# One pair of FFN columns fewer multiplied plainly, and the row scale's work queued ahead of the combinations

## The chip, the cores and the metric

One core of a Trainium2 chip. The time is in device microseconds (us), from start to end of one execution; the median of 3 runs counts. A profiled execution gives the trace.

## What is computed

One decoder layer, 512 tokens, width 1024, all in f32. The change touches the two half-step FFNs and the projection between them:

```python
h = h + 0.5 * swiglu(rms_norm(h, ln_ffn1), w1_gate, w1_up, w1_down)     # DFF = 2816
u = rms_norm(h, ln_mix) @ w_in                                          # recurrence and attention
h = h + concat([o_hgrn, o_mla]) @ w_out
h = h + 0.5 * swiglu(rms_norm(h, ln_ffn2), w2_gate, w2_up, w2_down)
h = h + sigmoid(rms_norm(h, ln_ple) @ w_ple_gate) * (p @ w_ple_proj)
y = rms_norm(h, ln_final)

def rms_norm(x, g): return x * rsqrt(mean(x * x) + 1e-6) * g            # per token
def swiglu(x, wg, wu, wd): return (silu(x @ wg) * (x @ wu)) @ wd
```

## The kernel before

**Layout and precision.** h lies transposed: 8 tiles of 128 features by 512 tokens. Every f32 factor is split into an upper half (ScalarE copies it to fp32r) and the rest (VectorE subtracts); a product is three matmuls, hi*hi, lo*hi, hi*lo (`mm3`, L226). Weights come from HBM in pieces of 8 blocks of 128x128 (`WStream`): 7 buffers for raw pieces (tag `wraw`), 3 for split ones (`whi`, `wlo`). L73 makes the upper half of a piece on ScalarE, L74 the rest on VectorE. A load goes out on SyncE when its buffer is free.

**Norm.** `Norm.add` (L295) scales a tile of h by the gain and splits it (L238, L239). `square` (L302) squares it on ScalarE and adds it to a running sum on VectorE. The factor per token is applied only after the product: `finish` (L327) sums over the features with four tiny matmuls (L268, tile `ss`) and takes the reciprocal root with a dozen 4-wide VectorE operations (`rsqrt_of`, L241 to L262). `row_bcast` (L343) spreads it: a diagonal, upper half (L275) and rest (L280), two matmuls with ones (L282, L283), and a copy to SBUF (L346, tile `rb`).

**FFN.** There are 22 column tiles of 128, taken in pairs. A plain pair is four products of gate and up columns, each of 8 slices of x of 3 matmuls of 512 columns, 96 in all. `plain_out` (L366) then forms gate times factor (L368), silu (L369), times up (L371), and splits it (L235, L236). A Strassen pair treats gate and up, two halves of the features and two halves of the tokens as a 2x2 block product, with 7 products (`product`, L374) of 24 matmuls of 256 columns. Its operands are combinations of weights (`_form`: T1 L101, T2 L104, T3 L107, T4 L110, on VectorE, 1024 wide) and of x (`forms`, L311: for each k from 0 to 3 one ScalarE copy, four VectorE operations L317 to L320, and two splits into tiles `sx`). `end_pair` (L402) collects them; c is read on VectorE at L416 before its second use (L382).

PSUM has three accumulators `acc`, three `t` and two `aux`. The first FFN computes three pairs plainly, the second two, and the rest by Strassen (`PLAIN`, L1045). After six pairs the first `down` follows, after eleven the second.

The opening of an FFN: tiles 0 and 1 (four accumulators `gu`) take the slices of x in the order MO; then come `finish`, tile 2 in steps of two slices, `row_bcast` after six of the eight, `plain_out` for tiles 0 and 1, and with the later tiles one or two of the groups of combinations. Tile 3's accumulators are those of tile 0, so its first matmul waits until VectorE has read the gate of tile 0 (L368), and its second accumulator until L371. In the first FFN the squares are taken after the loop over the slices (L559); in the second with each tile of h that w_out finishes (L946).

The order of the program is a Python program's. The framework's scheduler then moves instructions on each engine, by its own estimate of when they are ready; each engine runs its own list in order.

Of the kernel before, what the change touches and what calls it, by code (L numbers as in the profile page):

```python
# [10 lines left out]
F32 = mybir.dt.float32  # L11
# [3 lines left out]
AF = mybir.ActivationFunctionType  # L15
ALU = mybir.AluOpType
# [5 lines left out]
KD = D // P  # L22
# [9 lines left out]
MO = [0, 4, 1, 5, 2, 6, 3, 7]  # L32
# [7 lines left out]
class WStream:  # L40
# [104 lines left out]
    def next(self, n=1):  # L145
        if not self.left:
            self._fill()
            self.left = self.ready.pop(0)
        hi, lo, o, end = self.left[0]
        assert o + n <= end  # L150
        self.left = self.left[n:]
        s = slice(o * P, (o + n) * P)
        return hi[:, s], lo[:, s]
# [10 lines left out]
def block_kernel(ctx: ExitStack, tc: tile.TileContext, xT, pT, pos, wst, items, vecs, lnf, cmask, tmask, out):  # L164
    nc = tc.nc
    V, S, G, PE = nc.vector, nc.scalar, nc.gpsimd, nc.tensor
# [9 lines left out]
    def nm(s):  # L176
        count[0] += 1
        return f"{s}_{count[0]}"

    def slot(name, dt=F32):  # L180
        return slots.tile([P, T], dt, tag="slot", name=nm(name), bufs=NSLOT)

    def tmpt(name, tag="tmp", bufs=4):
        return tmp.tile([P, T], F32, tag=tag, name=nm(name), bufs=bufs)

    def acc(name):
        return ps.tile([P, T], F32, tag="acc", name=nm(name), bufs=3)

    def tps(name):
        return ps.tile([P, T], F32, tag="t", name=nm(name), bufs=3)  # L190

    def aslot(name, dt=F32):
        return slots.tile([P, T], dt, tag="a", name=nm(name), bufs=8)

    def aux(name):
        return ps.tile([P, T], F32, tag="aux", name=nm(name), bufs=2)
# [8 lines left out]
    ones = const.tile([P, 1], F32, name="ones")  # L205
# [6 lines left out]
    warm = const.tile([P, 1], F32, name="warm")  # L212
    S.activation(warm, ones, AF.Silu)
    ident = const.tile([P, P], F32, name="ident")
# [49 lines left out]
    def col_sums(sqs, out):  # L264

        for j in range(sqs[0].shape[1] // P):
            for i, sq in enumerate(sqs):
                PE.matmul(out[:, j:j + 1], sq[:, j * P:(j + 1) * P], ones,  # L268
                          start=(i == 0), stop=(i == len(sqs) - 1))

    def broadcast_ps(r):

        n = r.shape[1]
        hi, lo = (tmp.tile([P, T], F32R, tag="tmp", name=nm("dg"), bufs=4) for _ in range(2))
        V.tensor_tensor(hi[:, :n * P].rearrange("p (j t) -> p j t", j=n),  # L275
                        ident.unsqueeze(1).broadcast_to([P, n, P]),
                        r.unsqueeze(2).broadcast_to([P, n, P]), op=ALU.mult)
        for j in range(n):
            c = slice(j * P, (j + 1) * P)
            V.scalar_tensor_tensor(lo[:, c], ident, r[:, j:j + 1], hi[:, c].bitcast(F32), op0=ALU.mult, op1=ALU.subtract)  # L280
        b = aux("rbp")
        PE.matmul(b[:, :n * P], ones_r, hi[:, :n * P], start=True, stop=False)  # L282
        PE.matmul(b[:, :n * P], ones_r, lo[:, :n * P], start=False, stop=True)  # L283
        return b
# [58 lines left out]
    def row_bcast(r, tag):  # L343
        b = broadcast_ps(r)
        o = tmpt("rb", tag=tag, bufs=1) if tag == "rb" else slot(tag)
        S.activation(o, b, AF.Copy)  # L346
        return o

    def ffn(norm, next_norm, n_plain, first=None, extra=None):

# [2 lines left out]
        rb = None  # L355

        def gated(f, tmp_a):
            new = aslot if f % 12 < 4 else slot
            hi, lo = new("ah", F32R), new("al", F32R)
            if len(tmp_a.shape) == 3:  # L360
                split(tmp_a, hi.rearrange("p (two t) -> p two t", two=2), lo.rearrange("p (two t) -> p two t", two=2))
            else:
                split(tmp_a, hi, lo)
            a_hi[f], a_lo[f] = hi, lo

        def plain_out(f, g, u):  # L366
            gs = tmpt("gs")
            V.tensor_tensor(gs, g, rb, op=ALU.mult)  # L368
            S.activation(gs, gs, AF.Silu)  # L369
            a = tmpt("a")  # L370
            V.tensor_tensor(a, u, gs, op=ALU.mult)  # L371
            gated(f, a)
# [67 lines left out]
                if last:  # L440
                    next_norm.add(m)

        if first is None:
            first = [acc("gu"), tps("gu"), acc("gu"), tps("gu")]
            for k in MO:
                for u in first:
                    mm3(u, W.next(), norm.x(k), k == MO[0], k == MO[-1])
        g, u = acc("gu"), tps("gu")

        def plain_tile(n=KD):  # L450

            for i, k in enumerate(MO):
                for o in (g, u):
                    mm3(o, W.next(), norm.x(k), k == MO[0], k == MO[-1])
                if i % n == n - 1:
                    yield

        tile2 = plain_tile(2)
        r = norm.finish()
        S.activation(warm, ones, AF.Silu)  # L460
        for _ in range(3):
            next(tile2)
        rb = row_bcast(r, "rb")
        next(tile2)
        for f in range(2):
            plain_out(f, first[2 * f], first[2 * f + 1])
        forms = list(range(4))
        for f in range(2, 2 * n_plain):
            if f > 2:
                next(plain_tile())  # L470
            if forms:
                norm.forms(forms.pop(0))
            if n_plain == 2:
                norm.forms(forms.pop(0))
            plain_out(f, g, u)
            if f + 1 < 2 * n_plain:
                g, u = acc("gu"), tps("gu")
        d = {}
        begin = start_pair(d)
        for _ in begin:  # L480
# [70 lines left out]

    n1 = Norm(V_LN1)
    first = [acc("gu"), tps("gu"), acc("gu"), tps("gu")]
    for k in MO:
        n1.add(k, square=False)
        for u in first:
            mm3(u, W.next(), n1.x(k), k == MO[0], k == MO[-1])
    W.ahead = 3
    for k in range(KD):  # L559
        n1.square(k)  # L560
    nmix = Norm(V_LNM)
    ffn(n1, nmix, PLAIN[0], first, make_tables)
    cos, sin, lb, oml = (tables[n] for n in ("cos", "sin", "lb", "oml"))


# [11 lines left out]
    rb = rc = None  # L577
# [215 lines left out]
    rb = row_bcast(rc, "rb")  # L793
# [146 lines left out]
    n2 = Norm(V_LN2)  # L940
    for m in MO:
        u = acc("wo")
        for k in range(KD):
            mm3(u, W.next(), mix[k], k == 0, k == KD - 1)
        V.tensor_tensor(h[m], h[m], u, op=ALU.add)
        n2.add(m)  # L946


    n3 = Norm(V_LNP)
    ffn(n2, n3, PLAIN[1])  # L950


    pp = []
    for j in range(2):
        praw = aslot("praw")
        nc.sync.dma_start(praw, pT[j * P:(j + 1) * P, :])
        hi, lo = aslot("ph", F32R), aslot("pl", F32R)
# [84 lines left out]


GROUPS = {}
PLAIN = (3, 2)  # L1045
FORMS = ("T1", "B11", "B21", "T2", "T3", "B22", "T4")


def _stream(w1_gate, w1_up, w1_down, w_in, w_q_up, w_kv_up, w_out, w2_gate, w2_up, w2_down, w_ple_gate, w_ple_proj):
# [19 lines left out]
    def col(n):  # L1069
        return slice(n, n + P)  # L1070

    def ffn(n, g, u, d, sizes):
        plain([w[k * P:(k + 1) * P, col(f * P)] for k in MO for f in range(2) for w in (g, u)], sizes)
        plain([w[k * P:(k + 1) * P, col(f * P)] for f in range(2, 2 * PLAIN[n]) for k in MO for w in (g, u)])
        first = n * KF
        for p in range(PLAIN[n], KF // 2):
            GROUPS[first + p] = {
# [8 lines left out]

        forms(PLAIN[n], "T1", "B11")
        for p in range(PLAIN[n], KF // 2):
            forms(p, "B21", "T2")
# [90 lines left out]
```

## Time and profile before

| | us |
|---|---|
| median of 3 runs | 1024.57 (1023.31 to 1025.12) |
| profiled execution | 1024.24 |
| its span | 1022.5 |
| TensorE busy | 1007.6 |
| VectorE busy | 728.6 |
| ScalarE busy | 449.5 |

The span is counted from the first to the last instruction; all starts below are in us from its start. Busy times overlap between engines. Matmuls are pipelined, so one lasts longer in the list than the distance to the next: the distance is the cost. DVE is VectorE, ACT ScalarE, PE TensorE, PEld its weight loads, SP SyncE.

### The profile page before, as it was taken

To read this page: it belongs to the slowest core of one execution; us is meant where nothing else is said; L and a number is where in the kernel's file an instruction comes from. 1 tells how busy PE (TensorE), PEld (TensorE's weight loads), DVE (VectorE), ACT (ScalarE), POOL (GpSimd) and SP (SyncE) were. 2 spreads that over 40 slices of the span, in tenths; PEclk is the share of its full clock that TensorE was granted. 3 is DMA by queue.
4 is the path that set the end of the run, shared out by engine and by line. 5 is a ranking of instruction groups with operands and counts; after the bars stand their busy time and mean duration, and the time that the engine had idled before them with its cause. 6 is when DMAs were issued, how large, how long until landed. Compare 5 with 4: busy or idle time off the path is not lost.

```text
span 1022.5 us, 14842 instructions
## 1 busy us (share of the span) xinstructions
PE 1007.6 (99%) x5987; PEld 885.0 (87%) x5987; DVE 728.6 (71%) x1183; ACT 449.5 (44%) x694; POOL 4.6 (0%) x13
## 2 busy tenths in 40 slices
PE   9899999999999999999999999999999999999996
PEld 7789998899998888897777788999988999988885
DVE  7857975579877668765757667788744699766655
ACT  8435552145554332345544444555521355543443
POOL 0000000000000000000000000000000000000000
PEclk9999999999999999999999999999999999999998
DMA  8212353123344321222310222132432223443301
GB/s 332 63 62 83 89 170 110 62 83 104 108 142 126 99 93 52 73 78 68 104 62 1 76 89 83 42 120 88 146 102 83 83 83 104 138 136 98 103 21 62
DMA packets 28980, 97.68 MB, mean 96 GB/s; under 512 B 3456, under 2 KB 3456, under 8 KB 28912
## 3 DMA queue, kind: packets, MB, share of 16 engines
q1 hardware_dynamic: 28752, 96.25, 29.2%
q8 instruction: 47, 0.77, 0.3%
q0 software_dynamic: 160, 0.49, 0.2%
q14 instruction: 21, 0.17, 0.0%
HBM read 94.10 MB, written 2.10 MB: 94 GB/s over the span
## 4 chain that ended last, share of the span: by engine, by line
PE 93%; DVE 3%; issue 1%; DMA 1%; ACT 1%; SPq 0%; DVEq 0%; ACTq 0%
PE down L228 8%; PE down L229 8%; PE down L230 8%; PE a L384 6%; PE a L383 6%; PE a L382 6%; PE c L382 3%; PE c L384 3%; PE c L383 3%; PE gu L228 3%; PE gu L229 3%; PE gu L230 3%; PE b L384 2%; PE b L383 2%; PE b L382 2%; PE ufq L228 2%
## 5 line engine op out<-in xcount | busy, mean ns | idle before, releaser
L73 ACT ACTIVATE whi<-wraw 128x1024 fp32r<-128x1024 f32 (+1 forms) x220 | 230.1, 1046 | 388.4 <-PE down L229 85.7
L74 DVE TENSOR_TENSOR wlo<-wraw,whi 128x1024 fp32r<-128x1024 f32 (+1 forms) x220 | 265.1, 1205 | 85.1 <-ACT whi L73 84.3
L229 PE MATMUL down<-al,whi 128*128 128x512 f32 x352 | 137.1, 390 | 0.0
L228 PE MATMUL down<-ah,whi 128*128 128x512 f32 x352 | 137.1, 390 | 0.0
L230 PE MATMUL down<-ah,wlo 128*128 128x512 f32 x352 | 137.0, 389 | 0.0
L382 PE MATMUL c<-sx,whi 128*128 128x256 f32 x272 | 78.7, 289 | 0.6 <-DVE u L416 0.6
L228 PEld LDWEIGHTS down<-ah,whi 128*128 128x128 f32 x352 | 66.1, 188 | 14.2 <-ACT ah L235 0.7
L229 PEld LDWEIGHTS down<-al,whi 128*128 128x128 f32 x352 | 66.1, 188 | 13.7 <-DVE al L236 0.4
L230 PEld LDWEIGHTS down<-ah,wlo 128*128 128x128 f32 x352 | 66.1, 188 | 13.7
L384 PE MATMUL a<-x,wlo 128*128 128x256 f32 x272 | 77.0, 283 | 0.0
L384 PE MATMUL a<-sx,wlo 128*128 128x256 f32 x272 | 77.0, 283 | 0.0
L383 PE MATMUL a<-sx,whi 128*128 128x256 f32 x272 | 77.0, 283 | 0.0
L383 PE MATMUL a<-x,whi 128*128 128x256 f32 x272 | 77.0, 283 | 0.0
L382 PE MATMUL a<-sx,whi 128*128 128x256 f32 x272 | 77.0, 283 | 0.0
L384 PE MATMUL c<-sx,wlo 128*128 128x256 f32 x272 | 76.9, 283 | 0.0
L382 PE MATMUL a<-x,whi 128*128 128x256 f32 x272 | 76.9, 283 | 0.0
L383 PE MATMUL c<-sx,whi 128*128 128x256 f32 x272 | 76.9, 283 | 0.0
L228 PE MATMUL gu<-x,whi 128*128 128x512 f32 x160 | 63.5, 400 | 2.9 <-DVE gs L368 2.6
L229 PE MATMUL gu<-x,whi 128*128 128x512 f32 x160 | 62.9, 394 | 0.0
L230 PE MATMUL gu<-x,wlo 128*128 128x512 f32 x160 | 62.7, 393 | 0.0
L382 PEld LDWEIGHTS c<-sx,whi 128*128 128x128 f32 x272 | 52.0, 191 | 3.2 <-DVE u L416 2.6
L383 PEld LDWEIGHTS a<-x,whi 128*128 128x128 f32 x272 | 52.2, 192 | 0.1
(308 smaller groups left out, 2173.5 us busy)
## 6 DMA issues: line engine op xcount, KB each, us to landing
wraw<-wst SPq DMA_DIRECT2D x169, 512.0 KB, 3.4
h<-xT SPq DMA_DIRECT2D x8, 256.0 KB, 6.1
out<-y SPq DMA_DIRECT2D x8, 256.0 KB, 2.2
wraw<-wst SPq DMA_DIRECT2D x7, 256.0 KB, 2.7
rpb<-rpa SPq DMA_DIRECT2D x8, 64.0 KB, 2.1
praw<-pT SPq DMA_DIRECT2D x2, 256.0 KB, 3.4
gf<-lnf SPq DMA_DIRECT2D x2, 256.0 KB, 4.3
posi<-pos POOLq DMA_DIRECT2D x1, 256.0 KB, 4.3
```

The source lines that it names most:

```text
L73: self.nc.scalar.activation(hi, src, AF.Copy)
L74: self.nc.vector.tensor_tensor(lo, src, hi.bitcast(F32), op=ALU.subtract)
L228: PE.matmul(out, a[0], b[0], start=start, stop=False)
L229: PE.matmul(out, a[0], b[1], start=False, stop=False)
L230: PE.matmul(out, a[1], b[0], start=False, stop=stop)
L382: PE.matmul(o, hi[:, c], x[0], start=begin and i == 0 and k == 0, stop=False, skip_group_check=True)
L383: PE.matmul(o, hi[:, c], x[1], start=False, stop=False, skip_group_check=True)
L384: PE.matmul(o, lo[:, c], x[0], start=False, stop=end and i == 1 and k == 3, skip_group_check=True)
```

## The change

One pair more in each FFN goes by Strassen (`PLAIN` from (3, 2) to (2, 1)), 19 in place of 17. In the first FFN each tile's square is taken with the tile, the row sums come before the last slice, and the first group of combinations right behind them; the broadcast comes after four slices of tile 2, and groups 1 to 3 follow the outputs of tiles. In the second FFN the row sums come after one slice, the broadcast after six, still in tiles 0 and 1; three groups of combinations are made in w_out, after the tiles of h that they need, and the fourth behind the scale. `tc.issue_after` keeps those groups behind the last VectorE operation of the broadcast's diagonal in VectorE's list.

```diff
         for j in range(n):
             c = slice(j * P, (j + 1) * P)
-            V.scalar_tensor_tensor(lo[:, c], ident, r[:, j:j + 1], hi[:, c].bitcast(F32), op0=ALU.mult, op1=ALU.subtract)
+            chain_end[0] = V.scalar_tensor_tensor(lo[:, c], ident, r[:, j:j + 1], hi[:, c].bitcast(F32), op0=ALU.mult, op1=ALU.subtract)
...
-        if first is None:
-            first = [acc("gu"), tps("gu"), acc("gu"), tps("gu")]
-            for k in MO:
+        def behind(k):
+
+            with tc.issue_after(chain_end[0].ins):
+                norm.forms(k)
+
+        S.activation(warm, ones, AF.Silu)
+        if n_plain == 1:
+            first, forms = [acc("gu"), tps("gu"), acc("gu"), tps("gu")], [3]
+            for i, k in enumerate(MO):
+                if i == 1:
+                    r = norm.finish()
+                if i == 6:
+                    rb = row_bcast(r, "rb")
                 for u in first:
                     mm3(u, W.next(), norm.x(k), k == MO[0], k == MO[-1])
-        g, u = acc("gu"), tps("gu")
-
-        def plain_tile(n=KD):
-
+        else:
+            forms = [1, 2, 3]
+        for f in range(2, 2 * n_plain):
+            g, u = acc("gu"), tps("gu")
             for i, k in enumerate(MO):
+                if f == 2 and i == 4:
+                    rb = row_bcast(r, "rb")
+                    for e in range(2):
+                        plain_out(e, first[2 * e], first[2 * e + 1])
+                    behind(forms.pop(0))
                 for o in (g, u):
                     mm3(o, W.next(), norm.x(k), k == MO[0], k == MO[-1])
-                if i % n == n - 1:
-                    yield
-
-        tile2 = plain_tile(2)
-        r = norm.finish()
-        S.activation(warm, ones, AF.Silu)
-        for _ in range(3):
-            next(tile2)
-        rb = row_bcast(r, "rb")
-        next(tile2)
-        for f in range(2):
-            plain_out(f, first[2 * f], first[2 * f + 1])
-        forms = list(range(4))
-        for f in range(2, 2 * n_plain):
-            if f > 2:
-                next(plain_tile())
+            plain_out(f, g, u)
             if forms:
-                norm.forms(forms.pop(0))
-            if n_plain == 2:
-                norm.forms(forms.pop(0))
-            plain_out(f, g, u)
-            if f + 1 < 2 * n_plain:
-                g, u = acc("gu"), tps("gu")
+                behind(forms.pop(0))
+        if n_plain == 1:
+            behind(forms.pop(0))
+            for e in range(2):
+                plain_out(e, first[2 * e], first[2 * e + 1])
...
-    for k in MO:
-        n1.add(k, square=False)
+    for i, k in enumerate(MO):
+        n1.add(k)
+        if i == KD - 1:
+            r1 = n1.finish()
+            n1.forms(0)
         for u in first:
             mm3(u, W.next(), n1.x(k), k == MO[0], k == MO[-1])
     W.ahead = 3
-    for k in range(KD):
-        n1.square(k)
...
         n2.add(m)
+        if 4 <= m < 7:
+            n2.forms(m - 4)
...
-PLAIN = (3, 2)
+PLAIN = (2, 1)
```

TensorE's list at the end of tiles 0 and 1 of the first FFN, before (x_253 is the last slice of x, x_126 the first, here of tile 2):

```order
L230 MATMUL gu_124<-x_253,wlo_238 128x512
L228 MATMUL gu_125<-x_253,whi_237 128x512
L229 MATMUL gu_125<-x_253,whi_237 128x512
L230 MATMUL gu_125<-x_253,wlo_238 128x512
L268 MATMUL ss_293<-ones,ssum_268 128x1 x4
L228 MATMUL gu_291<-x_126,whi_317 128x512
```

and now (x_249 is the last slice but one, x_273 the last):

```order
L230 MATMUL gu_125<-x_249,wlo_258 128x512
L268 MATMUL ss_279<-ones,ssum_129 128x1 x4
L228 MATMUL gu_122<-x_273,whi_257 128x512
L229 MATMUL gu_122<-x_273,whi_257 128x512
L230 MATMUL gu_122<-x_273,wlo_258 128x512
L228 MATMUL gu_123<-x_273,whi_257 128x512
```

The row sums moved from behind the last slice to ahead of it.

VectorE's list in the first FFN from the end of the reciprocal root (ry) over the two diagonals (dg) to the first gate product (gs), before:

```order
L257 SCALAR_TENSOR_TENSOR ry_300<-ru_303,ry_300 128x4
L317 SCALAR_TENSOR_TENSOR sf_678<-h_78,vec,a_77_677 128x256
L74 TENSOR_TENSOR wlo_360<-wraw_357,whi_359 128x1024
L275 TENSOR_TENSOR dg_375<-ident,ry_300 128x512
L101 TENSOR_TENSOR wraw_619<-wraw_615,wraw_617 128x1024
L280 SCALAR_TENSOR_TENSOR dg_376<-ident,ry_300,dg_375 128x128 x4
L318 SCALAR_TENSOR_TENSOR sf_678<-h_74,vneg,sf_678 128x256
L319 SCALAR_TENSOR_TENSOR sf_678<-h_74,vec,a_77_677 128x256
L320 SCALAR_TENSOR_TENSOR sf_678<-h_78,vec,sf_678 128x256
L74 TENSOR_TENSOR wlo_446<-wraw_443,whi_445 128x1024
L368 TENSOR_TENSOR gs_399<-gu_122,rb_385 128x512
```

and now:

```order
L257 SCALAR_TENSOR_TENSOR ry_286<-ru_289,ry_286 128x4
L277 TENSOR_TENSOR dg_372<-ident,ry_286 128x512
L74 TENSOR_TENSOR wlo_345<-wraw_342,whi_344 128x1024
L282 SCALAR_TENSOR_TENSOR dg_373<-ident,ry_286,dg_372 128x128 x4
L319 SCALAR_TENSOR_TENSOR sf_403<-h_76,vec,a_47_402 128x256
L321 SCALAR_TENSOR_TENSOR sf_403<-h_72,vec,a_47_402 128x256
L320 SCALAR_TENSOR_TENSOR sf_403<-h_72,vneg,sf_403 128x256
L107 TENSOR_TENSOR wraw_473<-wraw_591,wraw_473 128x1024
L322 SCALAR_TENSOR_TENSOR sf_403<-h_76,vec,sf_403 128x256
L236 TENSOR_TENSOR sx_410<-sf_403,sx_409 128x512
L74 TENSOR_TENSOR wlo_420<-wraw_417,whi_419 128x1024
L370 TENSOR_TENSOR gs_384<-gu_122,rb_382 128x512
```

Between ry and the second diagonal stood a combination (sf), a weight piece (L74) and a formed weight (L101); now one piece does. The combinations, T3 (L107) and a piece stand between it and the gate product.

VectorE's list at the end of w_out, from the residual add of the last tile but one (h_74), before (x_5555 is the last x, its sum follows):

```order
L945 TENSOR_TENSOR h_74<-h_74,wo_5485 128x512
L74 TENSOR_TENSOR wlo_5527<-wraw_5524,whi_5526 128x1024
L239 SCALAR_TENSOR_TENSOR x_5517<-h_74,vec,x_5517 128x512
L309 TENSOR_TENSOR ssum_5293<-ssum_5293,sq_5520 128x512
L945 TENSOR_TENSOR h_78<-h_78,wo_5523 128x512
L74 TENSOR_TENSOR wlo_5568<-wraw_5565,whi_5567 128x1024
L239 SCALAR_TENSOR_TENSOR x_5555<-h_78,vec,x_5555 128x512
L309 TENSOR_TENSOR ssum_5293<-ssum_5293,sq_5558 128x512
```

and now (x_5696 is the last x, rv_5730 the first operation of the reciprocal root):

```order
L947 TENSOR_TENSOR h_74<-h_74,wo_5626 128x512
L236 TENSOR_TENSOR sx_5623<-sf_5612,sx_5622 128x512
L74 TENSOR_TENSOR wlo_5668<-wraw_5665,whi_5667 128x1024
L239 SCALAR_TENSOR_TENSOR x_5658<-h_74,vec,x_5658 128x512
L311 TENSOR_TENSOR ssum_5389<-ssum_5389,sq_5661 128x512
L947 TENSOR_TENSOR h_78<-h_78,wo_5664 128x512
L107 TENSOR_TENSOR wraw_5788<-wraw_5927,wraw_5788 128x1024
L239 SCALAR_TENSOR_TENSOR x_5696<-h_78,vec,x_5696 128x512
L311 TENSOR_TENSOR ssum_5389<-ssum_5389,sq_5699 128x512
L74 TENSOR_TENSOR wlo_5710<-wraw_5707,whi_5709 128x1024
L247 TENSOR_SCALAR rv_5730<-ss_5725 128x4
```

A low half (sx) came in ahead of the piece, T3 of the first Strassen pair (L107) came ahead of the last x, and a weight piece moved behind its sum.

## Rows read from the trace of the kernel before

**Rows 1.** The page, busy time, share of the span and instructions of each engine.
```profile
PE 1007.6 (99%) x5987; PEld 885.0 (87%) x5987; DVE 728.6 (71%) x1183; ACT 449.5 (44%) x694; POOL 4.6 (0%) x13
```

**Rows 2.** Waits of TensorE, whole span: us in total, times, longest.
```profile
PE gu L228 <- DVE gs L368: 2.6, 1, 2.6
...
PE c L382 <- DVE u L416: 0.6, 1, 0.6
```

**Rows 3.** TensorE timeline, first FFN: start, length, line, operation, idle before.
```profile
28.13 0.94 PE L268 MATMUL ss<-ones,ssum 128*128 128x1 f32 x8
...
28.93 0.49 PE L228 MATMUL gu<-x,whi 128*128 128x512 f32 x1
...
40.72 0.40 PE L230 MATMUL gu<-x,wlo 128*128 128x512 f32 x1
...
43.70 0.50 PE L228 MATMUL gu<-x,whi 128*128 128x512 f32 x1 [2.59 <-DVE gs L368]
...
78.11 0.28 PE L382 MATMUL c<-sx,whi 128*128 128x256 f32 x1
```

**Rows 4.** Stages: length; busy us (count) of PE, PEld, DVE, ACT, POOL; clock, DMA, GB/s.
```profile
5.00:20.00 15.00, 14.74 (x62) 11.89 (x62) 13.37 (x21) 13.11 (x21) 0.00 (x0) 1.00 1.02 394
...
44.00:48.00 4.00, 4.00 (x12) 3.10 (x12) 3.45 (x6) 2.17 (x4) 0.00 (x0) 0.57 0.45 131
...
100.00:120.00 20.00, 20.00 (x168) 19.84 (x167) 18.77 (x22) 10.88 (x14) 0.00 (x0) 1.00 0.36 106
```

**Rows 5.** TensorE timeline, second FFN, from its first matmul to the first Strassen product.
```profile
605.01 0.39 PE L228 MATMUL gu<-x,whi 128*128 128x512 f32 x1
...
626.77 0.95 PE L268 MATMUL ss<-ones,ssum 128*128 128x1 f32 x8
...
649.97 0.28 PE L382 MATMUL c<-sx,whi 128*128 128x256 f32 x1
```

**Rows 6.** VectorE timeline, the same operation of two successive Strassen pairs.
```profile
694.55 0.69 DVE L419 TENSOR_TENSOR u<-c,u 128x512 f32<-128x512 f32 x1 [0.96 <-PE c L384]
...
714.92 0.69 DVE L419 TENSOR_TENSOR u<-c,u 128x512 f32<-128x512 f32 x1 [0.63 <-PE c L384]
```

**Rows 7.** VectorE timeline, row scale and combinations, first FFN, then second.
```profile
29.86 0.15 DVE L247 TENSOR_SCALAR rv<-ss 128x4 f32<-128x4 f32 x1
...
37.27 0.69 DVE L275 TENSOR_TENSOR dg<-ident,ry 128x512 fp32r<-128x512 f32 x1
...
40.06 0.48 DVE L318 SCALAR_TENSOR_TENSOR sf<-h,vneg,sf 128x256 f32<-128x256 f32 x1
...
630.17 0.16 DVE L251 TENSOR_SCALAR ry<-ry 128x4 int32<-128x4 int32 x1
...
632.02 0.69 DVE L275 TENSOR_TENSOR dg<-ident,ry 128x512 fp32r<-128x512 f32 x1
```

**Rows 8.** ScalarE timeline, the start of the kernel, then the first gate.
```profile
4.14 0.71 ACT L238 ACTIVATE x<-h,vec 128x512 fp32r<-128x512 f32 x1
...
4.98 0.63 ACT L73 ACTIVATE whi<-wraw 128x512 fp32r<-128x512 f32 x1
...
8.55 0.61 ACT L305 ACTIVATE ssum<-h 128x512 f32<-128x512 f32 x1
...
42.30 1.28 ACT L369 ACT_TABLE_LOAD   x1
...
43.68 0.63 ACT L369 ACTIVATE gs<-gs 128x512 f32<-128x512 f32 x1
```

**Rows 9.** End of w_out: VectorE, SyncE, time of a load, and a later wait.
```profile
600.64 1.23 DVE L74 TENSOR_TENSOR wlo<-wraw,whi 128x1024 fp32r<-128x1024 f32 x1 [0.18 <-ACT whi L73]
...
601.89 0.33 SPq L63 DMA_DIRECT2D wraw<-wst  x1
...
DMA to landing us min/median/max: 3.2/3.3/4.3
...
665.72 1.23 DVE L104 TENSOR_TENSOR wraw<-wraw,wraw 128x1024 f32<-128x1024 f32 x1 [1.79 <-DMA wraw<-wst]
```

More of the change, by code (lines that the diff above doesn't have):

```diff
@@ L269, in col_sums @@
                           start=(i == 0), stop=(i == len(sqs) - 1))
+    chain_end = [None]
     def broadcast_ps(r):
@@ L347, in row_bcast, with ffn @@
         return o
-    def ffn(norm, next_norm, n_plain, first=None, extra=None):
+    def ffn(norm, next_norm, n_plain, first=None, r=None, extra=None):
         a_hi, a_lo = {}, {}
@@ L558, in block_kernel @@
     W.ahead = 3
-    for k in range(KD):
-        n1.square(k)
     nmix = Norm(V_LNM)
-    ffn(n1, nmix, PLAIN[0], first, make_tables)
+    ffn(n1, nmix, PLAIN[0], first, r1, make_tables)
     cos, sin, lb, oml = (tables[n] for n in ("cos", "sin", "lb", "oml"))
```

## Prediction

> **What bounds the kernel now.** The page comes first: TensorE is busy for 1007.6 of 1022.5 us and VectorE for 71% [rows 1]. A gain can therefore come only from fewer or shorter matmuls, or from the 15 us in which TensorE has nothing to do. The waits of TensorE say where these are: apart from start and end there is one wait of 2.6 us, for a VectorE product of the first FFN, and one of 0.6 us in the second [rows 2]. TensorE's timeline of the first FFN then shows the place [rows 3]: the row sums at 28.13, tile 2 from 28.93, nothing between 40.72 and 43.70, the first Strassen product at 78.11. The table by stage gives the granted clock behind the gap, 0.57 of full speed, part of the stretch at the lower of the two levels (1.2 GHz), and 1.00 elsewhere [rows 4]. The timelines of the second FFN and of the pairs give the prices [rows 5, 6]. VectorE's and ScalarE's timelines show why the gap is there and what the new order puts in its place [rows 7 to 9].
>
> The sum is made against the profiled execution, 1024.24 us (span 1022.5 and 1.7 around it). The median of the runs, 1024.57, lies 0.33 above; differences are carried over to it. A measurement of this kernel can tell about 0.2% (2 us) from no change.
>
> **One plain pair fewer in each FFN.** A plain pair is 4 tiles of 8 slices of 3 matmuls, 96 matmuls of 512 columns. The second FFN's opening has exactly these, from 605.01 to 626.77 [rows 5]: 21.76 us, 0.2267 each. A Strassen pair is 7 products of 24 matmuls, 168 of 256 columns. Two successive pairs are 714.92 - 694.55 = 20.37 us apart [rows 6]; the bare spacing is 20.00/168 = 0.119 us [rows 4], and 0.2 to 0.4 us per pair goes to the place where c is used again. Each pair saves 1.39 us, both 2.78.
> The price on the other engines is real: three more weight pieces to split and four combinations of weights, seven operations of 1.23 us [rows 9] on VectorE. It is covered by TensorE, since VectorE is busy 18.77 of 20 us in a pair with TensorE at 20.00 [rows 4]. Without that cover each microsecond over costs one. The bytes of weights are the same.
> The rows say 0.2267 and 0.119 us for the two widths. A rule speaks against the swap: the Trainium skill, TensorE: Matmul & The Clock Gate, section Back-to-back issue gap, has a stream of weight loads and matmuls sustained at about 81 ns for 128 columns and 131 ns for 512; read linearly, an estimate of 98 ns for 256 gives 168 x 0.098 = 16.5 against 96 x 0.131 = 12.6 us, 3.9 us lost per pair and a total near 1027.5. The trace has other spacings and decides.
>
> **The row scale in the first FFN.** Now the row sums stand after all 96 matmuls, and the dozen tiny operations behind them are mixed with combinations and pieces: 29.86 for the first, 37.27 for the diagonal of the result [rows 7], 7.4 us. Left alone, its last ten take 632.02 - 630.17 = 1.85 us [rows 7]. Tile 2 from 28.93 should take 48 x 0.2267 = 10.88 and 0.46 for the two broadcast matmuls; tile 3 starts at 43.70, 14.77 later: 3.43 us lost. From 43.70 to 78.11 the 144 matmuls of three tiles take 34.41 instead of 32.64: 1.77 us, the slow clock. Together 5.20.
> In the new order the row sums precede the last slice, 12 x 0.2267 = 2.72 us earlier, and only one weight piece stands inside the chain. I walk it with the opening 0.3 later (below). They stand at 28.13 + 0.3 - 2.72 = 25.7 and take 0.8, as now. VectorE finishes the formed weight T1 at 26.9, so the chain and the first diagonal end at 29.7. The piece between waits for its upper half, whose buffer TensorE releases at 29.1: ScalarE until 30.1, VectorE until 31.3. The second diagonal ends at 32.4. TensorE asks for it after four slices of tile 2, at 29.2 + 24 x 0.2267 = 34.7: 2.3 us to spare. The broadcast is copied at 36.3, after one more piece.
> Next in VectorE's queue, ahead of the product that frees tile 0's second accumulator: eight 256-wide combinations (0.48 long [rows 7], some 0.4 apart), the weight T3, one piece, two low halves and the first gate product. With the starts spaced as in the rows the freeing product ends between 40.1 and 40.9. Tile 3 asks for that accumulator at 40.55 + 0.68 = 41.2. So I take the whole 5.20, with 0.3 to 1.1 us to spare; this is the tightest place. Bounds of the gain: 5.20, and 0 where the same gap returns.
> The gate's table load lies here. In the trace it starts at 42.30 and the gate at 43.68, 1.38 us [rows 8], which the walk has room for. The Trainium skill, ScalarE: Activation LUTs, section What ACT_TABLE_LOAD costs, adds a drain of about 1.38 us, 2.66 in all; by that the product ends 0.3 to 1.1 us behind the need and the gain is that much smaller. No drain shows in the row.
>
> **Squares with each tile.** Number and length are the same; they only move forward. VectorE is busy for 13.37 of 15 us in the opening already [rows 4], and a slice of x, its sum and half a piece (about 0.7, 0.7 and 0.6 us) fit into the 2.72 us that TensorE needs for a slice: price 0 from the second slice on. On the first slice the square, 0.61 us, comes ahead of the first weight's upper half; x ends at 4.85 and that half starts at 4.98 [rows 8]. Bounds 0 and 0.61; I take 0.3, since the 0.1 between is free and successive ScalarE starts overlap by 0.1. Loss 0.3.
>
> **Combinations in w_out.** Three of four groups (four combinations, two low halves, some 3 us each) go into every second column block there, where VectorE waits for TensorE; the slack hides them: price 0, and up to 0.5 us of delay on a residual add that nobody waits for.
> One thing is new and is a wait: VectorE's T3 now stands between the last residual add and the last x. It needs quadrant B22, loaded into the buffer that a w_out piece leaves. That piece is split at 600.64 and its load issued at 601.89 [rows 9]; the combinations ahead make it about 602.6. Loads land after 3.2 to 4.3 us [rows 9]: 605.8 to 606.9. Behind T3 (1.13 to the next start) are the last x, 0.66, and the last sum, 0.69; TensorE wants the sum after 15 matmuls, at 605.01 + 3.40 = 608.4. It is ready between 608.3 and 609.4. Loss 0 to 1.0; I take 0.15, since the median load of 3.3 us is the nearest row.
> The scale itself has ample time: it is asked for after six of eight slices, some 13 us later. The former plain tiles of this FFN ran without gaps (605.01 to 649.97, 192 matmuls, row sums and broadcast: 44.96 against 44.8 [rows 5]), so nothing else is won here. The 0.6 us wait [rows 2] is the T2 of the second pair waiting 1.79 us for its load [rows 9]; the order there is unchanged, and I leave it.
>
> **Sum.** -5.20 - 2.78 + 0.30 + 0.15 = -7.5 us: 1016.7 in a profile, 1017.0 as a median.
>
> **Rivals.**
> 1. The gap returns smaller. If the freeing product in VectorE's queue comes more than the 0.3 to 1.1 us late, tile 3 waits again; at the full old price (2.75 of gap, 1.77 of clock) the time is 1021.5. For: twelve other operations precede it behind the diagonal. Against: each has its row.
> 2. T3's load is late in the second FFN. 1.0 us gives 1018; a gap as long as the old one, with its clock, 1021.4. Against: no load in this stretch took over 4.3 us.
> 3. Slower: VectorE sets the pace in the pairs. With 18.77 of 20 us it has little to spare, and if it enters the first pair late and each pair keeps a wait such as the 1.79 us on a load, TensorE waits where c is used again, in all 19 pairs. The kernel is slower by over 0.2% from a period of about 20.9 us; at 21.5 (18.77 scaled to the pair, and the waits of 1.79 and 0.6) it comes to about 1039. Against: the period was 20.37 in pair after pair, and TensorE did not wait.
> 4. Narrow matmuls lose. If in the two new pairs the weight loads set the spacing, at their mean of 885.0/5987 = 0.148 us [rows 1], a pair takes 168 x 0.148 = 24.9 us, 3.1 more than a plain one, and the time is 1017.0 + 2.8 + 6.2 = 1026. This is the direction of the TensorE page's rule of the Trainium skill. Against: in 17 pairs the loads overlapped, at 0.119.
> 5. Better: the first weight isn't delayed, T3 never waits and the 0.6 us goes too: 1016 and below.
>
> **How the numbers follow.** Forecast 0.72, with its own range 1015.9 to 1018.4. Rival 1: 0.11, rival 2: 0.09, rival 3: 0.04, rival 4: 0.01, rival 5 (under 1015.9): 0.03. The range reaches up over most of rivals 1 and 2 and down over part of 5: 1014.8 to 1020.8. Faster by over 0.2% is everything below 1022.5: the forecast, rival 5 and nearly all of 1 and 2, 0.92; within 0.2% a bad mixture of 1 and 2, 0.03, and rival 4, 0.04 together; slower rival 3, 0.04.
>
> **What would show it.** In the changed profile: no wait of TensorE for a gate product and no clock below 1.00 between 35 and 60 us; the first Strassen product near 51.6 instead of 78.11; 19 pairs 20.4 us apart; a wait for the row sums in the second FFN of 0 to 1 us; VectorE a little busier. The prediction is wrong where tile 3 waits for its second accumulator, where a pair is longer than 20.9 us, or where the waits on row sums pass 1 us.

## Result and profile after

The changed kernel takes 1017.04 us (median of 4 runs, 1016.25 to 1018.14) against 1024.57 before: a ratio of 0.993, interval 0.991 to 0.9949. A fourth run of the kernel before, of 2295.93 us, is left out of its median. The forecast was 1017.0, its range 1014.8 to 1020.8. The profiled execution is the longest of the four, 1018.14 us with a span of 1016.4. From profile to profile that is 6.1 us less, where the sum said 7.5; the difference is found in the opening.

Busy time by engine (changed kernel), then TensorE's waits: us in total, times, longest.

```profile
PE 1003.9 (99%) x6131; PEld 889.0 (87%) x6131; DVE 746.8 (73%) x1203; ACT 458.1 (45%) x706; POOL 4.6 (0%) x13
```

```profile
PE c L384 <- DVE u L418: 0.8, 1, 0.8
PE gu L228 <- ACT whi L73: 0.6, 1, 0.6
```

The wait of 2.6 us for a gate product [rows 2] is gone. The wait for the first weight has more than doubled (0.26 before), and the one at the point where c is used again is still there, in another pair.

TensorE's timeline of the changed kernel: start, length, line, operation.

```profile
26.86 0.95 PE L268 MATMUL ss<-ones,ssum 128*128 128x1 f32 x8
...
30.53 0.39 PE L228 MATMUL gu<-x,whi 128*128 128x512 f32 x1
...
41.89 0.39 PE L228 MATMUL gu<-x,whi 128*128 128x512 f32 x1
...
42.57 0.39 PE L228 MATMUL gu<-x,whi 128*128 128x512 f32 x1
...
52.77 0.28 PE L384 MATMUL c<-sx,whi 128*128 128x256 f32 x1
...
600.00 0.39 PE L228 MATMUL gu<-x,whi 128*128 128x512 f32 x1
...
603.49 0.72 PE L268 MATMUL ss<-ones,ssum 128*128 128x1 f32 x5
...
623.35 0.28 PE L384 MATMUL c<-sx,whi 128*128 128x256 f32 x1
...
1006.93 0.39 PE L230 MATMUL pj<-kh,pl 128*128 128x512 f32 x1
```

TensorE's last matmul in the kernel before:

```profile
1013.02 0.39 PE L230 MATMUL pj<-kh,pl 128*128 128x512 f32 x1
```

The rows of the changed kernel answer to [rows 3, 5]. Tile 2 begins at 30.53; tile 3 takes its first accumulator at 41.89 and its second at 42.57. The four stages of the difference can be read from them.

1. Opening. The row sums now stand ahead of the last slice, so tile 2 begins at 30.53, against 28.93 before: 1.60 us later, where the sum had 0.30.
2. From there to the first Strassen product: 52.77 - 30.53 = 22.24. Before it was 78.11 - 28.93 = 49.18, and 27.42 without the pair that was exchanged. Gain 5.18 (forecast 5.20).
3. From there to the second FFN: 547.23 now, 526.90 before. The Strassen pair that was added costs 20.33 where the plain one cost 21.76. Gain 1.43 (1.39).
4. Second FFN: 23.35 to the first Strassen product, against 44.96 - 21.76 = 23.20. Loss 0.15 (0.15). From there to the last matmul it is 383.58 now and 363.05 before: one pair of 20.53 more, which includes 0.2 of longer wait for c. Gain 1.23 (1.39).

Together 1.60 - 5.18 - 1.43 + 0.15 - 1.23 = -6.09.

VectorE's timeline of the changed kernel: the row scale of the first FFN, the end of w_out, and two successive pairs.

```profile
28.08 0.15 DVE L247 TENSOR_SCALAR rv<-ss 128x4 f32<-128x4 f32 x1
...
30.39 0.69 DVE L277 TENSOR_TENSOR dg<-ident,ry 128x512 fp32r<-128x512 f32 x1
...
38.24 0.68 DVE L370 TENSOR_TENSOR gs<-gu,rb 128x512 f32<-128x512 f32 x1
...
41.28 0.68 DVE L373 TENSOR_TENSOR a<-gu,gs 128x512 f32<-128x512 f32 x1
...
600.94 1.22 DVE L107 TENSOR_TENSOR wraw<-wraw,wraw 128x1024 f32<-128x1024 f32 x1
602.09 0.75 DVE L239 SCALAR_TENSOR_TENSOR x<-h,vec,x 128x512 fp32r<-128x512 f32 x1
602.75 0.68 DVE L311 TENSOR_TENSOR ssum<-ssum,sq 128x512 f32<-128x512 f32 x1
...
687.58 0.69 DVE L421 TENSOR_TENSOR u<-c,u 128x512 f32<-128x512 f32 x1 [0.96 <-PE c L386]
...
707.95 0.69 DVE L421 TENSOR_TENSOR u<-c,u 128x512 f32<-128x512 f32 x1 [0.96 <-PE c L386]
```

From the first tiny operation to the diagonal it is 2.3 us, against 7.4 in [rows 7]. The product that frees tile 0's second accumulator ends at 41.96. Tile 3 starts at 41.89 and takes that accumulator 0.68 later, at 42.57: 0.61 to spare, inside the forecast's 0.3 to 1.1. In the second FFN the last sum ends at 603.43; TensorE would have asked at 603.40 and starts at 603.49. A pair still takes 20.37.

ScalarE's timeline of the changed kernel, the opening and the first gate.

```profile
4.82 0.61 ACT L307 ACTIVATE ssum<-h 128x512 f32<-128x512 f32 x1
...
5.34 0.61 ACT L73 ACTIVATE whi<-wraw 128x512 fp32r<-128x512 f32 x1
...
38.02 1.28 ACT L371 ACT_TABLE_LOAD   x1
39.32 0.63 ACT L371 ACTIVATE gs<-gs 128x512 f32<-128x512 f32 x1
```

The square ahead of the first weight delays its upper half by 0.36 us (4.98 in [rows 8]), as taken. Of the 1.60, 0.34 is the later start of the first matmul (6.00 against 5.66). Another 0.15 only moved: the 12 matmuls behind the row sums take 2.87 us in place of 2.72 in both kernels, but in the kernel before they lie behind tile 2's start. The other 1.11 is TensorE's clock.

TensorE's first slices in the changed kernel, and the table by stage over the same stretch (length; busy us and count of PE, PEld, DVE, ACT, POOL; granted clock, DMA share, GB/s).

```profile
6.60 0.63 PE L229 MATMUL gu<-x,whi 128*128 128x512 f32 x1
7.02 0.63 PE L228 MATMUL gu<-x,whi 128*128 128x512 f32 x1
...
9.16 0.60 PE L229 MATMUL gu<-x,whi 128*128 128x512 f32 x1
9.58 0.41 PE L230 MATMUL gu<-x,wlo 128*128 128x512 f32 x1
9.83 0.40 PE L228 MATMUL gu<-x,whi 128*128 128x512 f32 x1
```

```profile
5.00:20.00 15.00, 14.39 (x55) 11.44 (x55) 14.03 (x20) 14.25 (x23) 0.00 (x0) 1.00 1.03 398
...
44.00:48.00 4.00, 4.00 (x19) 3.31 (x18) 4.00 (x8) 2.51 (x5) 0.00 (x0) 1.00 0.00 2
```

The starts are 0.43 us apart until 9.6, then 0.23. The first is the spacing at half clock, as the kernel before shows it in its slow stretch, where the clock column says 0.50 from 44.5 to 47.9:

```profile
46.20 0.63 PE L229 MATMUL gu<-x,whi 128*128 128x512 f32 x1
46.63 0.63 PE L230 MATMUL gu<-x,wlo 128*128 128x512 f32 x1
```

The second is the 0.2267 of full clock [rows 5]. In the opening the clock column says 1.00, even for 6.0 to 9.4 us alone, and doesn't show this; there the spacing of equal matmuls is the reading to trust. The slow stretch at 44 to 48, 0.57 in [rows 4], is gone.

### The profile page after: what moved, and what is told of

Read it like the earlier page. It is cut to its first block, busy times and chain, and to the rows that moved or that the text cites. A ratio compares the mean times of both kernels' runs of the same rounds, so it can differ in the third digit from the quotient of the medians.

```text
span 1016.4 us, 15166 instructions
## 1 busy us (share of the span) xinstructions
PE 1003.9 (99%) x6131; PEld 889.0 (87%) x6131; DVE 746.8 (73%) x1203; ACT 458.1 (45%) x706; POOL 4.6 (0%) x13
## 4 chain that ended last, share of the span: by engine, by line
PE 98%; DVE 1%; ACT 1%; issue 0%; DVEq 0%
PE down L228 8%; PE down L230 8%; PE down L229 8%; PE a L386 7%; PE a L385 7%; PE a L384 7%; PE c L384 4%; PE c L386 4%; PE c L385 4%; PE gu L228 2%; PE gu L229 2%; PE gu L230 2%; PE b L386 2%; PE b L385 2%; PE b L384 2%; PE ufq L228 2%
## 5 line engine op out<-in xcount | busy, mean ns | idle before, releaser
L73 ACT ACTIVATE whi<-wraw 128x1024 fp32r<-128x1024 f32 (+1 forms) x226 | 236.6, 1047 | 378.3 <-PE a L385 92.1
L74 DVE TENSOR_TENSOR wlo<-wraw,whi 128x1024 fp32r<-128x1024 f32 (+1 forms) x226 | 272.2, 1204 | 81.3 <-ACT whi L73 80.2
L384 PE MATMUL c<-sx,whi 128*128 128x256 f32 x304 | 87.9, 289 | 0.8 <-DVE u L418 0.8
L386 PE MATMUL a<-x,wlo 128*128 128x256 f32 x304 | 86.0, 283 | 0.0
L386 PE MATMUL a<-sx,wlo 128*128 128x256 f32 x304 | 86.0, 283 | 0.0
L385 PE MATMUL a<-sx,whi 128*128 128x256 f32 x304 | 86.0, 283 | 0.0
L385 PE MATMUL a<-x,whi 128*128 128x256 f32 x304 | 86.0, 283 | 0.0
L384 PE MATMUL a<-sx,whi 128*128 128x256 f32 x304 | 86.0, 283 | 0.0
L386 PE MATMUL c<-sx,wlo 128*128 128x256 f32 x304 | 86.0, 283 | 0.0
L385 PE MATMUL c<-sx,whi 128*128 128x256 f32 x304 | 86.0, 283 | 0.0
L384 PE MATMUL a<-x,whi 128*128 128x256 f32 x304 | 86.0, 283 | 0.0
L385 PEld LDWEIGHTS a<-x,whi 128*128 128x128 f32 x304 | 58.4, 192 | 0.1
L384 PEld LDWEIGHTS a<-x,whi 128*128 128x128 f32 x304 | 58.4, 192 | 0.1
L385 PEld LDWEIGHTS a<-sx,whi 128*128 128x128 f32 x304 | 58.4, 192 | 0.1
L384 PEld LDWEIGHTS a<-sx,whi 128*128 128x128 f32 x304 | 58.4, 192 | 0.1
```

The source lines that it names most:

```text
L73: self.nc.scalar.activation(hi, src, AF.Copy)
L74: self.nc.vector.tensor_tensor(lo, src, hi.bitcast(F32), op=ALU.subtract)
L384: PE.matmul(o, hi[:, c], x[0], start=begin and i == 0 and k == 0, stop=False, skip_group_check=True)
L385: PE.matmul(o, hi[:, c], x[1], start=False, stop=False, skip_group_check=True)
L386: PE.matmul(o, lo[:, c], x[0], start=False, stop=end and i == 1 and k == 3, skip_group_check=True)
```

## Experiments

Every kernel below was timed five or more times, with the kernel before beside it on the same chip (medians of that 1023.82, 1024.57 and 1024.59).

### Do the new order's two parts both matter?

The change moves the row sums forward, and it queues the combinations behind the row scale. Three kernels take these apart. The first drops the queue rule:

```diff
-            with tc.issue_after(chain_end[0].ins):
-                norm.forms(k)
+            norm.forms(k)
```

> The changed kernel without the rule that the combinations of x stand behind the row scale; the row sums stay ahead of the last slice. Theory (both parts are needed: without the rule four and more combinations, two low halves, a piece and a formed weight, about 5 us, stand between the dozen tiny operations): the second diagonal ends near 38 instead of 33.9, TensorE waits for it some 2 us, and then up to 1 us for the freeing product, the clock falls for a stretch: 1019 to 1021.5. Rival (the 2.7 us by which the row sums come earlier do it alone): within 0.5 us of the changed kernel, 1017.

1017.37 us (1016.43 to 1019.4), ratio 0.9938 [0.9925, 0.9951]: the rival. TensorE doesn't wait in the first FFN, though VectorE mixes the row scale with combinations and weights again, 7.0 us from the first tiny operation to the diagonal:

VectorE's timeline without the queue rule.

```profile
26.37 0.15 DVE L247 TENSOR_SCALAR rv<-ss 128x4 f32<-128x4 f32 x1
...
33.38 0.68 DVE L277 TENSOR_TENSOR dg<-ident,ry 128x512 fp32r<-128x512 f32 x1
...
36.94 0.69 DVE L370 TENSOR_TENSOR gs<-gu,rb 128x512 f32<-128x512 f32 x1 [0.30 <-ACT rb L348]
...
38.94 0.68 DVE L373 TENSOR_TENSOR a<-gu,gs 128x512 f32<-128x512 f32 x1
```

The second puts squares and row sums of the first FFN behind its first 96 matmuls and keeps the rule:

```diff
     for i, k in enumerate(MO):
-        n1.add(k)
-        if i == KD - 1:
-            r1 = n1.finish()
-            n1.forms(0)
+        n1.add(k, square=False)
         for u in first:
             mm3(u, W.next(), n1.x(k), k == MO[0], k == MO[-1])
+    for k in range(KD):
+        n1.square(k)
+    r1 = n1.finish()
+    n1.forms(0)
```

> The changed kernel with the squares and row sums of the first FFN taken after its first 96 matmuls, as before; the queue rule stays. Theory (both parts are needed: the row sums come 2.7 us later and the chain with them, while the freeing product has only 0.5 to 1.2 us to spare): TensorE waits some 2 us for the diagonal or the freeing product, and the clock falls for a stretch: 1019.5 to 1022. The opening gains 0.3 of that, since no square stands ahead of the first weight. Rival (the queue rule alone does it): 1016.7 to 1017.2.

1019.61 us (1018.79 to 1021.32), ratio 0.9955 [0.9943, 0.9967]. The size fits the theory, its mechanism doesn't: TensorE waits neither for the diagonal nor before tile 3. It waits later, in the first Strassen pair (at 73.75), for T2's load and what VectorE has behind it.

Waits of TensorE with late row sums; then VectorE's timeline there.

```profile
PE c L384 <- DVE u L418: 1.7, 2, 1.5
```

```profile
29.22 0.16 DVE L247 TENSOR_SCALAR rv<-ss 128x4 f32<-128x4 f32 x1 [0.96 <-PE ss L268]
...
37.68 0.69 DVE L370 TENSOR_TENSOR gs<-gu,rb 128x512 f32<-128x512 f32 x1
...
39.53 0.69 DVE L373 TENSOR_TENSOR a<-gu,gs 128x512 f32<-128x512 f32 x1 [0.17 <-ACT gs L371]
...
70.73 1.23 DVE L104 TENSOR_TENSOR wraw<-wraw,wraw 128x1024 f32<-128x1024 f32 x1 [1.96 <-DMA wraw<-wst]
...
73.01 0.68 DVE L418 TENSOR_TENSOR u<-c,u 128x512 f32<-128x512 f32 x1
```

The third has both edits:

> The changed kernel with both parts of the new order in the first FFN undone: no queue rule, and squares and row sums after the first 96 matmuls; the plain pairs stay at two and one, the combinations in w_out too. Theory (each part alone removes the gap, so only without both does it come back): TensorE waits 2.6 to 2.8 us for the gate product before tile 3, the clock falls to half behind it, the first Strassen product stands near 56 and the time is 1021 to 1022 (the old order with two and two pairs, 1022.8, less one exchanged pair of 1.4). Rival (the gap went for another reason): no wait there, 1017 to 1018.

1021.32 us (1019.82 to 1023.09), ratio 0.9963 [0.9951, 0.9975]. The gap and the slow clock are back.

TensorE's timeline with neither part, VectorE's, and the table by stage.

```profile
43.22 0.79 PE L228 MATMUL gu<-x,whi 128*128 128x512 f32 x1 [2.69 <-DVE gs L370]
```

```profile
29.21 0.16 DVE L247 TENSOR_SCALAR rv<-ss 128x4 f32<-128x4 f32 x1
...
42.48 0.68 DVE L370 TENSOR_TENSOR gs<-gu,rb 128x512 f32<-128x512 f32 x1
```

```profile
43.00:50.00 7.00, 6.78 (x17) 5.33 (x18) 6.80 (x11) 4.18 (x6) 0.00 (x0) 0.55 0.00 0
```

The rows of the four kernels give one account. In us from the first tiny operation, the table gives when the first gate product (the one that tile 3 waited for) ends and when tile 3 asks for its accumulator:

| kernel | product ends | tile 3 asks | late |
|---|---|---|---|
| neither part | 13.95 | 11.32 | 2.63 (waited 2.69) |
| queue rule alone | 9.15 | 11.65 | no |
| early row sums alone | 11.26 | 13.82 | no |
| both (the change) | 10.84 | 13.81 | no |

With neither part TensorE asks when it falls idle (43.22 - 2.69); in the others tile 3 starts without a wait, at 40.87, 40.19 and 41.89. Each part by itself covers the 2.63. The rule alone lets the product end 4.80 us sooner. Early row sums alone let tile 3 ask 2.50 later and the product end 2.69 sooner; the later asking by itself would have left 0.13 to wait. With early row sums the rule adds nothing that TensorE feels. It even leaves less to spare for the second accumulator: 0.61 us with both parts, against 1.25 with early row sums alone and 1.33 with the rule alone. With the rule alone the gap goes, but VectorE comes into the Strassen pairs later (the first T4, L110, starts 12.3 us after the first Strassen product, 6.1 in the changed kernel), and some of the gain is lost there: the time is 1.5 us above the changed kernel timed beside it (1018.08, below).

### The exchanged pair by itself

```diff
-PLAIN = (2, 1)
+PLAIN = (3, 1)
```

> The changed kernel with the third plain pair of the first FFN put back in the place of a Strassen pair; the new order of squares and combinations stays. Theory (a plain pair costs 21.76 us and a Strassen pair 20.37, and nothing else in the first FFN hangs on the swap): 1.4 us above the changed kernel, about 1018.4 us, no wait of TensorE in the first FFN, the first Strassen product some 21.8 us later. Rival (weight loads set the spacing of narrow matmuls): the plain pair is the shorter one, and the time falls by about 3, to 1014. Rival (the swap is what frees VectorE for the chain): the gap before tile 3 returns, 1020 or more.

1018.64 us (1017.34 to 1019.83), ratio 0.9955 [0.9943, 0.9968]. That is 0.6 above the changed kernel in its second series (1018.08) and 1.6 above the first: the direction and about the size of the theory, and against both rivals. Since both differences lie within the 2 us that a measurement tells, the profile has to show it. From the row sums to the first Strassen product this kernel takes 73.39 - 25.72 = 47.67, against 25.91: 21.76 for the plain pair. From there to the second FFN it takes 600.83 - 73.39 = 527.44, against 547.23: 19.79 for the Strassen pair, 0.5 less than in stage 3 above. By an estimate from its figures, the Trainium skill (TensorE: Matmul & The Clock Gate, section Back-to-back issue gap) would have made the plain pair the shorter one; the runs here show the opposite.

The same exchange in the kernel before, old order kept:

```diff
-PLAIN = (3, 2)
+PLAIN = (2, 2)
```

> The kernel before with one plain pair fewer in the first FFN; the order of its squares, row sums and combinations stays the old one. If the parts simply add: 1.4 us less than before, about 1023.2, with the old gap of 2.6 us before tile 3 and its slow stretch. Theory (the parts hang together: with one plain pair fewer the combinations of all four slices have two tiles fewer to hide in and stand ahead of the product that frees tile 0's accumulator, some four more combinations, two low halves and a piece, 4 us): the gap grows to some 6 us and the time to about 1027, so that the swap alone would have made the kernel slower.

1022.76 us (1020.33 to 1024.14, 11 runs), ratio 0.9989 [0.998, 0.9998]. My theory fell: as far as 2 us can tell, the parts add. The gap stays at 2.7 us; VectorE reaches the first gate product at 42.63, and at 42.97 in the kernel before, so nearly the same work stands ahead of it.

Waits of TensorE, old order with two plain pairs.

```profile
PE gu L228 <- DVE gs L368: 2.7, 1, 2.7
```

### The opening

Here I looked for the 1.60 us. The first try takes each square one slice later:

```diff
-        n1.add(k)
-        if i == KD - 1:
+        n1.add(k, square=False)
+        if i:
+            n1.square(MO[i - 1])
+        if i == KD - 1:
+            n1.square(k)
             r1 = n1.finish()
```

> The changed kernel, each square of the first FFN taken one slice later, so that no square stands ahead of the first weight's upper half; the row sums stay ahead of the last slice. Theory A (the square ahead costs 0.3 us, and the later rise of the clock in the profiled run, at 9.6 instead of 7.0 us, followed from the longer wait of 0.61 us before the first matmul): first matmul at 5.66 again, wait 0.26, spacing 0.23 us from about 7.0 us on, the row sums 1.4 us earlier, time 1.0 to 1.4 us below the changed kernel. Theory B (only the 0.3 us is the change's, the clock rises early or late from run to run, whatever the kernel): 0.3 us below in the median, and the rise at either place.

1017.26 us (1017.09 to 1019.38), ratio 0.9946 [0.9933, 0.9958]: not faster. In the profile the first load of h landed later, so the first matmul started at 5.93 all the same, and the clock rose only at 9.9.

The second try fills the pause before the first real matmul:

```diff
-WARM = 9
+WARM = 10
```

> The changed kernel with ten warm-up matmuls of TensorE instead of nine, so that TensorE is busy until 5.87 us instead of 5.40; the first real matmul can start at 6.0 as in the changed kernel. Theory A (the clock's late rise comes from the wait): the wait shrinks to 0.15 us or less, the spacing is 0.23 us from about 7 us on, time 0.8 to 1.1 us below the changed kernel. Theory B (the rise varies by itself): same time as the changed kernel within 0.5 us, the rise at either place.

1016.92 us (1016.49 to 1017.11), ratio 0.9938 [0.9924, 0.9952].

TensorE's timeline with ten warm-up matmuls.

```profile
5.93 0.50 PE L228 MATMUL gu<-x,whi 128*128 128x512 f32 x1 [0.83 <-ACT whi L73]
6.27 0.39 PE L229 MATMUL gu<-x,whi 128*128 128x512 f32 x1
6.50 0.40 PE L228 MATMUL gu<-x,whi 128*128 128x512 f32 x1
```

The matmuls are 0.23 apart from the start, and the row sums come at 25.11. But theory A can't be the whole of it: the wait got longer (0.83), because the clock had risen among the warm-up matmuls, ten in 3.91 us where nine took 4.21. So the changed kernel was run again, and ten and eight warm-up matmuls too:

> The changed kernel itself, for a second profile and five more times beside the next three. If the rise of the clock in the opening varies from run to run: a profile in which the spacing of 0.43 us ends elsewhere than at 9.6 us, and a median of 1016.5 to 1017.5. If it belongs to the kernel: the rise at 9.6 us again.

1018.08 us (1016.08 to 1018.57), ratio 0.9935 [0.9923, 0.9948].

> The changed kernel with ten warm-up matmuls, once more. If the tenth matmul makes the clock rise early each time: five runs within 0.8 us again, median 1016.5 to 1017.1, row sums near 25.1 in the profile. If that was chance: a spread of 2 us or more, as in the changed kernel, and a rise anywhere between 4 and 10 us.

1016.73 us (1016.44 to 1017.57), ratio 0.9925 [0.9913, 0.9938].

> The changed kernel with eight warm-up matmuls, TensorE idle for some 1 us before the first real one. If the pause decides when the clock rises: always late, row sums near 27, median 1018 to 1018.6. If it is chance: the median and spread of the changed kernel, 1016.1 to 1018.6.

1018.57 us (1017.39 to 1019.43), ratio 0.9939 [0.9927, 0.9952].

The profiles of the kernels with the change's opening, one execution each:

| kernel | warm-up | first matmul | 0.23 us apart from | row sums | first Strassen product |
|---|---|---|---|---|---|
| the change | 9 in 4.21 | 6.00 | 9.6 | 26.86 | 52.77 |
| the change again | 9 in 4.21 | 5.93 | 10.4 | 27.19 | 53.10 |
| no queue rule | 9 in 3.92 | 5.97 | the first | 25.14 | 51.07 |
| one more raw buffer (below) | 9 in 3.80 | 5.99 | the first | 25.16 | 51.08 |
| ten warm-ups | 10 in 3.91 | 5.93 | the first | 25.11 | 51.02 |
| ten again | 10 in 4.37 | 5.94 | the first | 25.16 | 51.07 |
| eight | 8 in 3.78 | 6.04 | 9.3 | 26.78 | 52.69 |
| three plain pairs (above) | 9 in 4.21 | 5.93 | the first | 25.72 | 73.39 |

The last row has one plain pair more, and a load of h that landed late (1.07 us of wait on ScalarE) cost it some 0.6 us. Otherwise the same opening ends at two places some 1.7 to 2 us apart, by whether the clock is up at the first real matmul or rises only behind the first slices; with nine warm-up matmuls both happen. Ten gave the early rise in both profiles and ten runs within 1016.44 to 1017.57; eight the late one and a median of 1018.57; the nine runs of the change spread from 1016.08 to 1018.57. A pause of TensorE that keeps the clock low was my guess, but its length alone doesn't decide. With nine warm-up matmuls in 4.21 us and the same pause of 0.53 us behind them, the clock was up at the first matmul in one profile (three plain pairs) and only at 10.4 us in another (the change again). Where it had risen among the warm-up matmuls, pauses of 0.83 to 1.00 us did not undo it. With one profile per series, what sets the moment stays open.

Both edits together:

> The changed kernel with each square one slice later and ten warm-up matmuls. If the opening's losses are the wait for the first weight and a clock that rises late when TensorE pauses: first matmul at 5.6 to 5.9, the clock up by 6.5 us in the profile, row sums at 25.0, median 1016.3 to 1016.9. If the clock's rise is a matter of chance: 1016.5 to 1018, with the spread of the changed kernel (2.5 us).

1017.42 us (1016.98 to 1018.08), ratio 0.9931 [0.9918, 0.9943]. The first matmul stands at 5.59, but the row sums only at 25.94: the second slice's weight is split at 8.31, where it was 7.16 in the changed kernel, because its load landed late.

TensorE and ScalarE with both edits.

```profile
8.31 0.63 ACT L73 ACTIVATE whi<-wraw 128x512 fp32r<-128x512 f32 x1 [1.32 <-DMA wraw<-wst]
...
9.00 0.50 PE L228 MATMUL gu<-x,whi 128*128 128x512 f32 x1 [0.39 <-ACT whi L73]
```

Late loads stand in the openings of other kernels too: ScalarE waited 0.68 us for this one with eight warm-up matmuls, and 0.97 us for one of h in the kernel before. Whether this one was late by chance stays open. The two series with later squares show no gain of the 0.36 us.

### The wait where c is used again

The 0.8 us in the pairs is VectorE waiting 1.86 us for a quadrant, for T2; from there to the operation that TensorE waits for (L418) it works without a gap:

VectorE's timeline of the changed kernel, late in the second FFN.

```profile
826.68 1.23 DVE L104 TENSOR_TENSOR wraw<-wraw,wraw 128x1024 f32<-128x1024 f32 x1 [1.86 <-DMA wraw<-wst]
...
831.23 0.68 DVE L418 TENSOR_TENSOR u<-c,u 128x512 f32<-128x512 f32 x1
```

```diff
-NRAW = 7
+NRAW = 8
```

> The changed kernel with eight buffers for raw weights instead of seven. Theory (the wait of 0.3 to 1.0 us where c is used again, in one or two of the 19 pairs, is the load of a quadrant that is issued only when a piece leaves its buffer, and then lands late): the wait is gone and the time falls by 0.3 to 0.8 us, to about 1016.4. Rival (the load is late by its own length or by traffic): the wait stays.

1017.69 us (1017.52 to 1019.77), ratio 0.9941 [0.9929, 0.9953]. My theory fell: VectorE waits for T2's load in 2 pairs instead of 17 (6.9 us in place of 17.0), but its 9 waits for T1's have grown from 5.0 to 9.9 us, and TensorE waits more than before.

Waits with eight raw buffers: TensorE's, VectorE's.

```profile
PE c L384 <- DVE u L418: 2.3, 5, 0.7
```

```profile
DVE wraw L101 <- DMA wraw<-wst: 9.9, 9, 2.2
```

In the changed kernel only one of the 17 waits for T2 reaches TensorE. An extra buffer moves the late load to another formed weight: in the pair with the longest wait for T1, 2.2 us, L418 follows it at once, and TensorE waits 0.6. What order of loads would end it wasn't tried.

The best version is the change with ten warm-up matmuls: 1016.92 and 1016.73 us, ratios 0.9938 and 0.9925. It is faster than the kernel before beyond doubt; from the changed kernel it can't be told apart, since 0.1 to 1.4 us lie within the 2 us that a measurement tells.

## Why the prediction was right

**The exchanged pairs** (2.78): 1.43 and 1.23 in the profiles, the second with a longer wait for c in it. The spacing of narrow matmuls was read from the pairs that were already there, and the added ones ran the same. VectorE covers the extra weights; rival 3 didn't come (a pair of 20.37), nor did rival 4. The 1.43 holds the combinations in w_out too, so their price of 0 shows no error.

**The row scale** (5.20): 5.18, of which 0.15 only moved into the opening. The size was right, because the walk through VectorE's queue counted each operation that stands ahead of the freeing product, and 0.61 us of the spare time was left. What it gave as the reason was half right. It spoke of tiny operations mixed with combinations, and took the unmixing for needed; the run without the rule shows the mixing again and no gap. The earlier row sums are enough, and so is the unmixing by itself. The walk also named the second accumulator as what decides. In the old order it was the first: there TensorE takes four slices of tile 3 and a matmul more for one accumulator before it turns to the other, and waits for the first gate product [rows 2]. In the new one the two accumulators alternate and the second is the tighter.

**The opening** (0.30): the term that was mis-sized. The 0.36 us at the first weight is there, but the profiles with this opening put tile 2's start 1.60 us later than before, or 0.1 earlier (28.82 without the queue rule), by when the clock rises. The prediction has no term for that: it read one profile of before, where the clock was up by 7.0 us, and its clock column, 1.00. The medians lie between the two, so the total still came out. That the first of them meets the forecast of 1017.0 so closely is luck: the same kernel timed again has 1018.08, and the profile's gain is 6.1 us, not 7.5.

**w_out and the second FFN** (0.15, bounds 0 to 1.0): 0.15. T3's load had landed by 600.94, and the last sum missed TensorE by 0.03 us.

**The table load** is followed by the gate 1.30 us after its start (38.02, 39.32), 0.02 after its end, with no drain behind it. The 1.38 in the prediction is not the load's own: there the gate also waited for its product, which ended at 43.65. By the Trainium skill, ScalarE: Activation LUTs, section What ACT_TABLE_LOAD costs, the gate would have stood some 1.36 us later, and the product with its 0.61 us to spare would have come late; the trace doesn't agree.

## What to carry to other kernels

Of a wait, write down two numbers from one starting point: when the awaited product ends and when it is asked for. Several edits can each close the difference, so undo them one by one and all together before you credit any. Before you trust a term about the first 10 us, look at the spacing of equal matmuls in more than one profile.

## What the runs showed of the hardware

The clock at the start rises at different moments in kernels with the same opening: among the nine warm-up matmuls (3.80 us instead of 4.21), by the first real matmul, or at 9.6 to 10.4 us, which moves everything behind it by up to 2 us. The clock column shows 1.00 there all the same. After a pause of 2.6 to 2.7 us TensorE ran at half clock, 1.2 GHz, for a while each time, but not equally long: to 47.9 us in the kernel before, to 47.3 in the old order with two plain pairs, and in the kernel with neither part to 49.4 (0.55 over 43 to 50). The changed kernel, which has no such gap, had no such stretch, and behind the 1.5 us wait with late row sums (at 73.75) the narrow matmuls stood 0.12 us apart from the second on.
